# Up products of a gated MLP with the high and low part of the rows as one 512-column moving operand

## The chip, the cores and the metric

The kernel runs on one core of a Trainium2 chip. The metric is device time in microseconds (us): the median of the runs of the whole program.

## The reference, cut to what matters

The program computes a decoder trunk of two layers over 256 rows (T) of width 1024 (D), with d_ff = 2816. Each layer is an attention part (one combined input projection, two attention mixers, two branch products, an output product) followed by a gated MLP with a causal convolution of width 3 behind the up-projection. The change is in the MLP, with two small moves outside it.

```python
def conv_ffn(h, w_up, conv_w, conv_b, w_down):
    u = h @ w_up
    s = u.shape[1]
    up = jnp.pad(u, ((0, 0), (CONV_WIDTH - 1, 0), (0, 0)))
    c = conv_b
    for k in range(CONV_WIDTH):
        c = c + conv_w[k] * up[:, k:k + s]
    a, val = jnp.split(c, 2, axis=-1)
    return (jax.nn.gelu(a, approximate=True) * val) @ w_down

x = x + rms_norm(mix, attn_post_gain)
h = rms_norm(x, ffn_pre_gain)
x = x + rms_norm(conv_ffn(h, ...), ffn_post_gain)
```

## The kernel before, in words

Every float32 product is emulated: each operand is split into a high part (rounded to the engine's fast fp32 form) and a low part (what is left), and three products are summed in PSUM: high·high, high·low and low·high. A weight tile comes by DMA, ScalarE casts its high part `wh` (L114, function `copy`), and VectorE subtracts to get its low part `wl` (L117, `sub`). These pairs `wh`, `wl` stand in a ring of four. A cast into a place of the ring waits for TensorE's last use of the tile that stood there four tiles earlier.

The MLP (`ffn_layer`) has the 2816 inner columns in 22 tiles of 128, numbered j. Each j has two halves (the gate's side and the value's side), each with a weight tile of its own of 8 x 128 x 128.

- j = 0 and 1 are made in another manner (`up_first`, rows as the stationary operand, then transposes).
- For j = 2 to 20: `up(j, 0)`, `up(j, 1)`, then the gate `act_gate`, then `down(j - 2)` for both blocks of 128 rows (t = 0, 1). `up` issues for each of 8 k-steps three matmuls of 256 columns (L1064: wh with the rows' high part `hh`; L1065: wh with the rows' low part `hl`; L1066: wl with `hh`). The result is transposed: 128 inner columns on partitions, 256 rows along the free axis, both halves of a j in one PSUM bank ("T" and "mm" in turn).
- The gate: for each half a convolution, which is one ACT instruction (L1047, scale and bias) and two VectorE instructions (L1050, L1051), all reading PSUM; gelu (L1073, ACT), the product of both halves (L1077, VectorE), the high part `gh` (L114, ACT) and the low part `gl` (L117, VectorE). `gh` and `gl` are the stationary operands of `down`, 12 matmuls of 512 columns for each j (L388 to L390), summed over all j into two banks "S" (t = 0) and two banks "O" (t = 1).
- j = 21 is done last, written out by hand (`manual_schedule`). Then `down` of j = 18 to 21 follows. In layer 0 the hand order stays in force to the end: t = 0 of all four, then t = 1. In the last layer the scheduler orders them.

After the products of a row block comes its norm: ACT squares and sums (L407), VectorE multiplies by the gain (L408) and adds to X (L413). In `out_layer`, ahead of the MLP, L384 squares X for the next norm, L984 scales it, L395 transposes it, and L114/L117 write the transposed rows' high and low parts (`hp`). `W.high(n)` issues a cast of weight tile n and returns the function that issues its low part.

At the start of layer 0, `rope_tables` builds the rotary tables `tab` (8 instructions on GpSimd, L370 and L371, from a cosine and a sine that ACT wrote); L502 and L504 on VectorE multiply q and k with them.

The order of the instructions on each engine is fixed when the program is built (a scheduler's list order except under `manual_schedule`); at run time each engine takes its instructions in that order.

Of the kernel before, what the change touches and what calls it, by code (L numbers as in the profile page):

```python
# [65 lines left out]
def tile_hybrid_trunk(  # L66
# [147 lines left out]
    TAGS = {"kB": 1, "sg": 2, "q8": 3}  # L214
# [71 lines left out]
    last_sq = [None]  # L286

# [60 lines left out]
    def rope_tables():  # L348
        pf = small("r_pf", 2, 1)
        dve.tensor_copy(pf, pos_i)  # L350
        tmp = k1().rearrange("p (i t d) -> p i t d", i=4, t=2)
        r, n, s, c = [tmp[:, i] for i in range(4)]
# [11 lines left out]
        dve.tensor_scalar(n, n, -1.0, math.pi / 2, ALU.mult, ALU.add)  # L364
# [78 lines left out]
    def attn_layer(l, xp, rs, gains, first, order, last_T):  # L443
# [16 lines left out]
        def in_tile(i, tag, fin, tmajor=False, hooks={}):  # L460
# [4 lines left out]
            def go(t, c):  # L465
                if c not in chs:
                    chs[c] = W.next(2, w)
# [93 lines left out]
        qA, qB, qR = big8("q8", 3), big8("q8", 3), big8("q8", 3)  # L561
# [398 lines left out]
        return yp  # L960

    def out_layer(l, yp, gains, order):
# [34 lines left out]
        hp = big8("q8", 3), big8("q8", 3)  # L997
# [29 lines left out]
        return hp, [lambda: t4_of(xg[1], hp, 1, 0), lambda: t4_of(xg[1], hp, 1, 1)]  # L1027


    def ffn_layer(l, hp, gains, last, order, last_T):  # L1030
        hh, hl = hp
# [12 lines left out]
        def conv(b, jj, half, then=None):  # L1044
            c = k1()
            u = b[:, half * T:(half + 1) * T]
# [72 lines left out]
        def up_first_T(t, us):  # L1119
# [97 lines left out]
    def start():  # L1217
# [31 lines left out]
        def rest():  # L1249
# [3 lines left out]
            rope_tables()  # L1253
# [94 lines left out]
```

## Time and profile before

| | |
|---|---|
| device time, median of 3 runs | 774.85 us (774.59 to 775.27) |
| profiled execution | 775.03 us |
| its span in the trace | 773.2 us |
| TensorE busy | 756.6 us, 98% of the span, mean granted clock 0.997 |
| VectorE busy | 611.8 us, 79% |
| ScalarE busy | 495.7 us, 64% |
| GpSimd busy | 33.1 us, 4% |
| MLP loop of layer 0 | 210 to 375.78 us |

The span is what the trace covers; the execution's time is 1.83 us longer. Engines are PE (TensorE matmul), PEld (its weight load), DVE (VectorE), ACT (ScalarE), POOL (GpSimd), SP (SyncE, DMA issue). Matmuls are pipelined, so the duration in a row is longer than the distance from one start to the next; the text counts distances of starts for them. A row of a timeline gives start, duration, engine, line, operation, output<-inputs, form, count, and in brackets how long the engine sat idle before it and who ended that.

### The profile page before, as it was taken

The page shows a single profiled execution, that of the slowest core. Times are in us where ns is not written, and L with a number is a line of the kernel's source. Part 1 is how long each engine was busy: PE and PEld are TensorE (multiplying, and loading weights), DVE is VectorE, ACT ScalarE, POOL GpSimd, SP SyncE. Part 2 cuts the span into 40 slices and gives each one's busy share as a digit, 9 for nine tenths or more (in the row PEclk, how much of TensorE's full clock was granted, in tenths as well). Part 3 has the DMA queues.
Part 4 walks back from the last instruction along what each step waited for, and adds up shares of the span by engine and source line. Part 5 has one row for each costly group of instructions (what it writes and reads, how often), then busy time and mean ns, then how long its engine had stood idle before and what let it go on. Part 6 is the DMA issues. An engine that isn't in the chain of part 4 may idle for free.

```text
span 773.2 us, 12869 instructions
## 1 busy us (share of the span) xinstructions
PE 756.6 (98%) x4742; PEld 676.7 (88%) x4742; DVE 611.8 (79%) x1180; ACT 495.7 (64%) x950; POOL 33.1 (4%) x60
## 2 busy tenths in 40 slices
PE   8999999999999999999999999999999999999996
PEld 6788898888799999999878889988888999999995
DVE  7899898687687777787787989985976876777675
ACT  6596987755565555665566979866565655566552
POOL 4200001000000000000010000010010000000000
PEclk9999999999999999999999999999999999999998
DMA  8624265355566565676335323544655565557631
GB/s 332 205 82 134 68 200 196 133 174 183 190 195 190 189 189 177 224 250 197 131 116 167 97 82 124 202 153 158 198 186 164 186 181 184 188 191 218 202 98 54
DMA packets 42346, 131.26 MB, mean 170 GB/s; under 512 B 5375, under 2 KB 5931, under 8 KB 42283
## 3 DMA queue, kind: packets, MB, share of 16 engines
q1 hardware_dynamic: 41707, 129.39, 51.9%
q10 hardware_dynamic: 576, 1.05, 0.4%
q8 instruction: 37, 0.61, 0.3%
q14 instruction: 26, 0.21, 0.1%
HBM read 129.37 MB, written 1.05 MB: 169 GB/s over the span
## 4 chain that ended last, share of the span: by engine, by line
PE 83%; ACT 8%; DVE 5%; issue 1%; POOL 1%; DMA 1%; SPq 0%; DVEq 0%; POOLq 0%; ACTq 0%
PE mm L388 6%; PE mm L390 6%; PE mm L389 6%; PE mm L1066 5%; PE mm L1065 5%; PE mm L1064 5%; PE S L388 5%; PE S L390 5%; PE S L389 5%; PE T L1065 5%; PE T L1064 5%; PE T L1066 5%; PE O L389 4%; PE O L388 4%; PE O L390 4%; PE T L674 2%
## 5 line engine op out<-in xcount | busy, mean ns | idle before, releaser
L117 DVE TENSOR_TENSOR wl<-st,wh 128x1024 fp32r<-128x1024 f32 (+2 forms) x214 | 253.5, 1185 | 96.0 <-ACT wh L114 95.2
L114 ACT ACTIVATE wh<-st 128x1024 fp32r<-128x1024 f32 (+2 forms) x214 | 218.8, 1027 | 160.5 <-PE mm L1065 39.3
L1064 PE MATMUL mm<-q,wh 128*128 128x256 f32 x336 | 95.1, 283 | 0.0
L1065 PE MATMUL mm<-q,wh 128*128 128x256 f32 x336 | 95.0, 283 | 0.0
L1066 PE MATMUL mm<-q,wl 128*128 128x256 f32 x336 | 95.0, 283 | 0.0
L388 PE MATMUL mm<-wh,x 128*128 128x512 f32 (+2 forms) x240 | 89.6, 373 | 0.7 <-DVE VT L558 0.7
L389 PE MATMUL mm<-wl,x 128*128 128x512 f32 (+2 forms) x240 | 88.3, 368 | 0.0
L390 PE MATMUL mm<-wh,x 128*128 128x512 f32 (+2 forms) x240 | 88.2, 368 | 0.0
L1065 PE MATMUL T<-q,wh 128*128 128x256 f32 x304 | 86.0, 283 | 0.0
L1066 PE MATMUL T<-q,wl 128*128 128x256 f32 x304 | 86.0, 283 | 0.0
L1064 PE MATMUL T<-q,wh 128*128 128x256 f32 x304 | 85.9, 283 | 0.0
L1064 PEld LDWEIGHTS mm<-q,wh 128*128 128x128 f32 x336 | 64.4, 192 | 1.0
L1065 PEld LDWEIGHTS mm<-q,wh 128*128 128x128 f32 x336 | 64.4, 192 | 0.8
L1066 PEld LDWEIGHTS mm<-q,wl 128*128 128x128 f32 x336 | 64.4, 192 | 0.1
L1064 PEld LDWEIGHTS T<-q,wh 128*128 128x128 f32 x304 | 58.3, 192 | 0.8
L1065 PEld LDWEIGHTS T<-q,wh 128*128 128x128 f32 x304 | 58.3, 192 | 0.7
L1066 PEld LDWEIGHTS T<-q,wl 128*128 128x128 f32 x304 | 58.3, 192 | 0.0
L388 PEld LDWEIGHTS mm<-wh,x 128*128 128x128 f32 x240 | 45.2, 188 | 5.7 <-issue 0.9
L390 PEld LDWEIGHTS mm<-wh,x 128*128 128x128 f32 x240 | 45.1, 188 | 5.6 <-DVE x L117 0.4
L389 PEld LDWEIGHTS mm<-wl,x 128*128 128x128 f32 x240 | 45.2, 188 | 4.5
L647 ACT ACTIVATE k<-k,mn 128x128 f32<-128x128 f32 (+1 forms) x96 | 42.4, 445 | 7.2 <-DVE mn L644 7.0
L114 ACT ACTIVATE k<-k 128x256 fp32r<-128x256 f32 x72 | 29.1, 414 | 14.6 <-DVE k L506 6.3
(336 smaller groups left out, 1672.1 us busy)
## 6 DMA issues: line engine op xcount, KB each, us to landing
st<-in_ffn_w_up_dram SPq DMA_DIRECT2D x88, 512.0 KB, 3.9
st<-in_ffn_w_down_dram SPq DMA_DIRECT2D x44, 512.0 KB, 3.6
st<-in_w_in_dram SPq DMA_DIRECT2D x42, 512.0 KB, 3.6
st<-in_w_out_dram SPq DMA_DIRECT2D x16, 512.0 KB, 3.8
st<-in_w_in_dram SPq DMA_DIRECT2D x16, 384.0 KB, 3.1
st<-in_cmp_w_dram SPq DMA_DIRECT2D x16, 256.0 KB, 2.6
st<-in_w_branch_a_dram SPq DMA_DIRECT2D x8, 512.0 KB, 3.6
st<-in_w_branch_b_dram SPq DMA_DIRECT2D x8, 512.0 KB, 3.5
```

The source lines that it names most:

```text
L114: return act.activation(dst, src, AF.Copy, scale=scale)
L117: return dve.tensor_tensor(dst, a, b, ALU.subtract)
L388: pe.matmul(o, xh, wh, start=first, stop=False, skip_group_check=True)
L389: pe.matmul(o, xh, wl, start=False, stop=False, skip_group_check=True)
L390: pe.matmul(o, xl, wh, start=False, stop=last, skip_group_check=True)
L647: last_exp[0] = act.activation(self.pt[:, hh, s, :], sm[:, :nk], AF.Exp, bias=self.mn[:, i:i + 1], scale=-1.0, accum_out=self.dn[:, i:i + 1])
L674: pe.transpose(b[:, i * P:(i + 1) * P], self.pt[:, h, s, kb * P:(kb + 1) * P], ident)
L1064: pe.matmul(o, wh[:, k, :], hh[:, k, c0:c1], start=(k == 0), stop=False, skip_group_check=True)
L1065: pe.matmul(o, wh[:, k, :], hl[:, k, c0:c1], start=False, stop=False, skip_group_check=True)
L1066: pe.matmul(o, wl[:, k, :], hh[:, k, c0:c1], start=False, stop=(k == 7), skip_group_check=True)
```

## The change

1. One tile `H` (128 x 2 x 8 x 256) holds the rows' high part `H[:, 0]` and low part `H[:, 1]`. In `up` each k-step issues one matmul of wh with both, 512 columns (one PSUM bank: columns 0 to 255 take high·high, 256 to 511 take high·low), and one of wl with `hh`, 256 columns into the first half. Each (j, half) has a bank of its own.
2. `left(j, half)`: ACT copies the bank's second half to SBUF, VectorE adds the first half to it. The convolution reads that sum in SBUF. For j = 0 and 1 nothing is added.
3. `act_gate(j)` issues both copies and adds, then both convolutions, then gelu, product, `gh`, `gl`.
4. `out_layer`: the cast of weight tile first+12 (`W.high`) is issued behind the second row block's squares, its low part behind the second transposes.
5. `rope_tables`: three ACT Sin instructions write `tab` themselves and one VectorE instruction makes the scaled pair; the GpSimd instructions are gone. The first weight tiles of in_tile 1 are issued behind that.

```diff
-        def up(j, half, c0, c1):
-            if j not in up_bank:
-                up_bank[j] = bank("T" if j % 4 < 2 else "mm")
+        def up(j, half):
+            b = up_bank[j, half] = bank("mm" if j % 2 == 0 else "T")
...
-            o = up_bank[j][:, half * T + c0:half * T + c1]
+            both = b.rearrange("p (s t) -> p s t", s=2)
             for k in range(8):
-                pe.matmul(o, wh[:, k, :], hh[:, k, c0:c1], start=(k == 0), stop=False, skip_group_check=True)
-                pe.matmul(o, wh[:, k, :], hl[:, k, c0:c1], start=False, stop=False, skip_group_check=True)
-                pe.matmul(o, wl[:, k, :], hh[:, k, c0:c1], start=False, stop=(k == 7), skip_group_check=True)
+                pe.matmul(both, wh[:, k, :], H[:, :, k, :], start=(k == 0), stop=False, skip_group_check=True)
+                pe.matmul(b[:, 0:T], wl[:, k, :], hh[:, k, :], start=False, stop=(k == 7), skip_group_check=True)
...
+        def left(j, half):
+            if j < 2:
+                return up_bank[j][:, half * T:(half + 1) * T]
+            b = up_bank.pop((j, half))
+            u = k1()
+            copy(u, b[:, T:2 * T])
+            dve.tensor_tensor(u, b[:, 0:T], u, ALU.add)
+            return u
+
+        def act_gate(j):
+            ua, uv = left(j, 0), left(j, 1)
+            ca, cv = conv(ua, j), conv(uv, 22 + j)
+            act.activation(ca, ca, AF.Gelu_apprx_tanh)
             dve.tensor_tensor(ca, ca, cv, ALU.mult)
...
-        low = W.high(first + 12)
         for n in range(2):
             norm_b(1, n, g, r)
-        low()
         r = rstd_of(mean_sq(halves(X[:, 1, :])))
+        low = W.high(first + 12)
...
-        act.activation(s, r, AF.Sin)
-        act.activation(c, n, AF.Sin)
-        for i, f in ((0, -SCALE), (2, 1.0)):
-            for h, g in ((0, -f), (1, f)):
-                dd = slice(h * 32, h * 32 + 32)
-                pool.tensor_scalar(tab[:, i, :, dd], c, f, None, ALU.mult)
-                pool.tensor_scalar(tab[:, i + 1, :, dd], s, g, None, ALU.mult)
+        twice = tab[:, 2].rearrange("p t (h d) -> p t h d", h=2)
+        act.activation(twice, c[:, :, None, :].to_broadcast([P, 2, 2, 32]), AF.Sin)
+        act.activation(tab[:, 3, :, 0:32], r, AF.Sin, scale=-1.0)
+        act.activation(tab[:, 3, :, 32:64], r, AF.Sin)
+        return angles, dve.tensor_scalar(tab[:, 0:2], tab[:, 2:4], -SCALE, None, ALU.mult)
```

Three places show how the instructions stand. First ScalarE in the middle of layer 0's MLP loop, before (a period of one j; `wh` rows are casts of weight tiles, `k` rows with L1047 the convolutions, L1073 gelu, the `k<-k` copy is `gh`):

```order
L1047 ACTIVATE k_669_2715<-mm_2654,vec 128x256
L114 ACTIVATE wh_2824<-st_2822 128x1024
L1073 ACTIVATE k_669_2715<-k_669_2715 128x256
L1047 ACTIVATE k_670_2720<-mm_2654,vec 128x256
L114 ACTIVATE wh_2843<-st_2841 128x1024
L114 ACTIVATE k_671_2725<-k_669_2715 128x256
```

And now (the copies out of banks T are `left`; the convolution is L1049, gelu L1081):

```order
L114 ACTIVATE wh_2954<-st_2952 128x1024
L114 ACTIVATE k_702_2848<-T_2802 128x256
L114 ACTIVATE k_703_2851<-T_2825 128x256
L114 ACTIVATE wh_2973<-st_2971 128x1024
L1049 ACTIVATE k_704_2854<-k_702_2848,vec 128x256
L1049 ACTIVATE k_705_2858<-k_703_2851,vec 128x256
L114 ACTIVATE wh_2996<-st_2994 128x1024
L1081 ACTIVATE k_704_2854<-k_704_2854 128x256
L114 ACTIVATE k_706_2864<-k_704_2854 128x256
```

The two copies are new, and the gate's work stands about one cast later against the casts than before. Second, ScalarE at the end of layer 0's MLP, before, from the last cast that waits for TensorE (`wh_4342`) to the last `gh` (`k_934`); the first L1047 is that of j = 20, half 0, L1155 is gelu of j = 21:

```order
L114 ACTIVATE wh_4342<-st_4340 128x1024 [waits DMAHW6_49,PE_49]
L1047 ACTIVATE k_917_4318<-T_4257,vec 128x256 [waits PE_49]
L1073 ACTIVATE k_917_4318<-k_917_4318 128x256 [waits DVE_49,Activation_49]
L1047 ACTIVATE k_918_4323<-T_4257,vec 128x256
L114 ACTIVATE k_919_4328<-k_917_4318 128x256 [waits DVE_49]
L1047 ACTIVATE k_928_4371<-T_4346,vec 128x256 [waits PE_49]
L1155 ACTIVATE k_928_4371<-k_928_4371 128x256 [waits DVE_49,Activation_49]
L1047 ACTIVATE k_930_4401<-mm_4376,vec 128x256 [waits PE_49]
L114 ACTIVATE wh_4405<-st_4403 128x1024
L114 ACTIVATE k_934_4411<-k_928_4371 128x256
```

And now, from j = 19's gate, behind that same cast (here `wh_4160`), through j = 20 (from `k_967`) to the first instruction of j = 21 (`k_980`); the rows of j = 21 go on as copy, convolution, gelu L1158, copy, convolution, a cast, `gh`:

```order
L114 ACTIVATE wh_4160<-st_4158 128x1024 [waits DMAHW6_49,PE_49]
L1049 ACTIVATE k_952_4052<-k_950_4046,vec 128x256 [waits DVE_49]
L1049 ACTIVATE k_953_4056<-k_951_4049,vec 128x256 [waits DVE_49]
L1081 ACTIVATE k_952_4052<-k_952_4052 128x256 [waits DVE_49,Activation_49]
L114 ACTIVATE k_954_4062<-k_952_4052 128x256 [waits DVE_49]
L114 ACTIVATE k_967_4130<-mm_4084 128x256
L114 ACTIVATE k_968_4133<-mm_4107 128x256 [waits PE_49]
L1049 ACTIVATE k_969_4136<-k_967_4130,vec 128x256 [waits DVE_49]
L1049 ACTIVATE k_970_4140<-k_968_4133,vec 128x256 [waits DVE_49]
L1081 ACTIVATE k_969_4136<-k_969_4136 128x256 [waits DVE_49,Activation_49]
L114 ACTIVATE k_971_4146<-k_969_4136 128x256 [waits DVE_49]
L114 ACTIVATE k_980_4181<-T_4164 128x256 [waits PE_49]
```

Behind that cast stood one and a half gates (j = 20 and 21, of which half 0 of j = 20 starts at once); now a gate more (19) stands there. Third, TensorE at the end of the last layer, before (`S` are the banks of t = 0, `O` those of t = 1, `k_1851` is `gh` of j = 21, `k_1811` that of j = 18):

```order
L388 MATMUL O_6962<-wh_8641,k_1811_8447 128x512
L389 MATMUL O_6962<-wl_8642,k_1811_8447 128x512
L390 MATMUL O_6962<-wh_8641,k_1812_8448 128x512
L388 MATMUL O_6963<-wh_8641,k_1811_8447 128x512
L388 MATMUL S_6954<-sg_8261,k_1851_8711 128x512 [waits Activation_49]
```

And now (`k_1945` is `gh` of j = 20, `k_1959` that of j = 21):

```order
L389 MATMUL O_6757<-kB_7756,k_1945_8265 128x512
L390 MATMUL O_6757<-kB_7756,k_1946_8266 128x512
L388 MATMUL S_6748<-sg_7929,k_1959_8333 128x512 [waits Activation_49]
L389 MATMUL S_6748<-sg_7930,k_1959_8333 128x512
L390 MATMUL S_6748<-sg_7929,k_1960_8334 128x512 [waits DVE_49]
L388 MATMUL S_6749<-sg_7929,k_1959_8333 128x512
L389 MATMUL S_6749<-sg_7930,k_1959_8333 128x512
L390 MATMUL S_6749<-sg_7929,k_1960_8334 128x512
L388 MATMUL O_6756<-sg_7929,k_1959_8333 128x512
```

All products of t = 1 for j = 18 to 20 now stand ahead of the first product of j = 21; before, four of them did.

## Rows read from the trace of the kernel before

**Rows 1.** The page's busy times, share of the span, instructions

```profile
PE 756.6 (98%) x4742; PEld 676.7 (88%) x4742; DVE 611.8 (79%) x1180; ACT 495.7 (64%) x950; POOL 33.1 (4%) x60
```

**Rows 2.** Windows, one j of layer 0: us, then busy us by engine, clock, DMA

```profile
242.12:250.65 8.53, 8.53 (x62) 8.01 (x61) 6.19 (x9) 4.72 (x7) 0.00 (x0) 1.00 0.62 185
```

**Rows 3.** Timeline of PE, next j: first product of each run

```profile
250.65 0.39 PE L388 MATMUL S<-wh,k 128*128 128x512 f32 x1
...
253.43 0.28 PE L1064 MATMUL mm<-q,wh 128*128 128x256 f32 x1
...
259.18 0.39 PE L388 MATMUL S<-wh,k 128*128 128x512 f32 x1
```

**Rows 4.** Timeline of PE, long run of 512 columns: first, and the 25th

```profile
14.50 0.39 PE L388 MATMUL mm<-wh,x 128*128 128x512 f32 x1
...
19.94 0.39 PE L388 MATMUL S<-wh,x 128*128 128x512 f32 x1
```

**Rows 5.** Timeline of PE, the dearest single step of 512 columns there

```profile
378.56 0.40 PE L388 MATMUL S<-kB,k 128*128 128x512 f32 x1
378.81 0.40 PE L389 MATMUL S<-kB,k 128*128 128x512 f32 x1
```

**Rows 6.** The page's groups of L1064: count, busy us, mean ns

```profile
L1064 PE MATMUL mm<-q,wh 128*128 128x256 f32 x336 | 95.1, 283 | 0.0
...
L1064 PE MATMUL T<-q,wh 128*128 128x256 f32 x304 | 85.9, 283 | 0.0
```

**Rows 7.** Groups by line, 210 to 364 us: count, busy us, mean ns, idle before

```profile
L117 DVE TENSOR_TENSOR wl<-st,wh 128x1024 fp32r<-128x1024 f32 x55 | 67.3, 1224 | 27.6 <-ACT wh L114 27.5
L114 ACT ACTIVATE wh<-st 128x1024 fp32r<-128x1024 f32 x54 | 57.1, 1058 | 47.8 <-PE mm L1065 19.2 <-PE O L390 15.8 <-PE T L1065 12.9
...
L1047 ACT ACTIVATE k<-mm,vec 128x256 f32<-128x256 f32 x19 | 10.4, 549 | 0.0
L1050 DVE SCALAR_TENSOR_TENSOR k<-mm,vec,k 128x255 f32<-128x255 f32 x19 | 9.1, 478 | 0.0
...
L1077 DVE TENSOR_TENSOR k<-k,k 128x256 f32<-128x256 f32 x19 | 8.1, 425 | 0.7
...
L114 ACT ACTIVATE k<-k 128x256 fp32r<-128x256 f32 x19 | 7.9, 416 | 2.5 <-DVE k L1077 2.4
```

**Rows 8.** Timeline of ACT, end of layer 0's MLP

```profile
370.10 1.06 ACT L114 ACTIVATE wh<-st 128x1024 fp32r<-128x1024 f32 x1 [1.49 <-PE T L1065]
...
380.24 0.42 ACT L114 ACTIVATE k<-k 128x256 fp32r<-128x256 f32 x1 [0.58 <-DVE k L1160]
```

**Rows 9.** Timeline of PE, same stretch

```profile
375.78 0.39 PE L388 MATMUL S<-wh,k 128*128 128x512 f32 x1
...
380.70 0.51 PE L388 MATMUL S<-sg,k 128*128 128x512 f32 x1 [0.58 <-ACT k L114]
```

**Rows 10.** Timeline of PE, end of the last layer

```profile
755.61 0.39 PE L388 MATMUL S<-wh,k 128*128 128x512 f32 x1
...
766.55 0.40 PE L390 MATMUL O<-sg,k 128*128 128x512 f32 x1
```

**Rows 11.** Timeline of DVE, end of the last layer

```profile
762.36 1.39 DVE L408 TENSOR_TENSOR k<-S,gain 128x512 f32<-128x512 f32 x2 [1.44 <-ACT k L407]
764.10 1.41 DVE L413 SCALAR_TENSOR_TENSOR X<-k,rstd,X 128x512 f32<-128x512 f32 x2 [0.34 <-POOL rstd L377]
...
768.73 1.41 DVE L413 SCALAR_TENSOR_TENSOR X<-k,rstd,X 128x512 f32<-128x512 f32 x2 [0.33 <-POOL rstd L377]
```

**Rows 12.** Timeline of ACT, end of layer 0's out_layer

```profile
198.88 1.05 ACT L114 ACTIVATE wh<-st 128x1024 fp32r<-128x1024 f32 x1
199.83 0.61 ACT L384 ACTIVATE k<-X 128x512 f32<-128x512 f32 x1
```

**Rows 13.** Timeline of PE, same stretch

```profile
203.10 0.63 PE L395 MATMUL T<-cst,k 128*128 128x128 f32 x4 [0.94 <-DVE k L984]
```

**Rows 14.** Timeline of POOL, rotary tables

```profile
23.86 1.35 POOL L370 TENSOR_SCALAR tab<-k 128x64 f32<-128x64 f32 x4
```

**Rows 15.** Timeline of DVE, first use of the tables

```profile
24.59 0.75 DVE L502 SCALAR_TENSOR_TENSOR k<-mm,rstd,tab 128x512 f32<-128x512 f32 x1 [1.59 <-POOL tab L370]
```

More of the change, by code (lines that the diff above doesn't have):

```diff
@@ L212, in next @@
             return self.made[self.used - 1]
-    TAGS = {"kB": 1, "sg": 2, "q8": 3}
+    TAGS = {"kB": 1, "sg": 2, "q8": 1}
     W = Stream()
@@ L286, in tile_hybrid_trunk @@
     last_sq = [None]
+    tables = []
     def table(fn):
@@ L351, in rope_tables @@
         tmp = k1().rearrange("p (i t d) -> p i t d", i=4, t=2)
-        r, n, s, c = [tmp[:, i] for i in range(4)]
+        r, n, c = [tmp[:, i] for i in range(3)]
         for t in range(2):
@@ L363, in rope_tables @@
         dve.scalar_tensor_tensor(n, r, -1.0, r, ALU.mult, ALU.max)
[L364 to L371 removed]
+        angles = dve.tensor_scalar(c, n, -1.0, math.pi / 2, ALU.mult, ALU.add)
+        twice = tab[:, 2].rearrange("p t (h d) -> p t h d", h=2)
[3 more added lines that the diff above has]
+        return angles, dve.tensor_scalar(tab[:, 0:2], tab[:, 2:4], -SCALE, None, ALU.mult)
     def rstd_of(s2):
@@ L466, in go @@
                 if c not in chs:
-                    chs[c] = W.next(2, w)
+                    with tc.issue_after(tables[c > 0].ins) if first and i == 1 else nullcontext():
+                        chs[c] = W.next(2, w)
                 ch = chs[c]
@@ L559, in v_split @@
             done.update(keys)
-        qA, qB, qR = big8("q8", 3), big8("q8", 3), big8("q8", 3)
+        H = ap_.tile([P, 2, KD, T], F32R, tag="h16", name=nm("H"))
+        qA, qB, qR = H[:, 0], H[:, 1], big8("q8", 1)
         kA = ap_.tile([P, 2, 2, T], F32R, tag="kA", name=nm("kA"))
@@ L959, in attn_layer, with out_layer @@
         branch(1)
-        return yp
-    def out_layer(l, yp, gains, order):
+        return yp, H
+    def out_layer(l, yp, H, gains, order):
         gains["ffn_pre"] = gain_tile(ffn_pre_gain, l)
@@ L996, in out_layer @@
             product(0, [k])
-        hp = big8("q8", 3), big8("q8", 3)
+        hp = H[:, 0], H[:, 1]
         g, r = norm_a(res[0], gp)
@@ L1019, in out_layer, with ffn_layer @@
             table(AF.Gelu_apprx_tanh)
-        low = W.high(first + 12)
         for n in range(2):
             norm_b(1, n, g, r)
-        low()
         r = rstd_of(mean_sq(halves(X[:, 1, :])))
+        low = W.high(first + 12)
         xg[1] = k4()
         scaled(1, r)
-        return hp, [lambda: t4_of(xg[1], hp, 1, 0), lambda: t4_of(xg[1], hp, 1, 1)]
-    def ffn_layer(l, hp, gains, last, order, last_T):
-        hh, hl = hp
+        return [lambda: t4_of(xg[1], hp, 1, 0), lambda: (t4_of(xg[1], hp, 1, 1), low())]
+    def ffn_layer(l, H, gains, last, order, last_T):
+        hh, hl = hp = H[:, 0], H[:, 1]
         gains["ffn_post"] = gain_tile(ffn_post_gain, l)
@@ L1042, in ffn_layer, with conv @@
         lows = []
-        def conv(b, jj, half, then=None):
+        def conv(u, jj, then=None):
             c = k1()
-            u = b[:, half * T:(half + 1) * T]
             act.activation(c, u, AF.Identity, bias=cb(l, jj), scale=cw(l, 2, jj))
@@ L1127, in up_first_T @@
                 for j in range(2):
-                    for half in range(2):
-                        act_gate(j, half)
+                    act_gate(j)
         for t in range(2):
@@ L1137, in ffn_layer @@
             for half in range(2):
-                part(lambda: up(j, half, 0, T))
-            for half in range(2):
-                act_gate(j, half)
+                part(lambda: up(j, half))
+            act_gate(j)
             if j in (NJ - 8, NJ - 6):
@@ L1152, in ffn_layer @@
             W.ensure(early[l, k])
-        part(lambda: up(j, 0, 0, T))
-        ca = conv(up_bank.pop(j), j, 0)
+        part(lambda: up(j, 0))
+        ca = conv(left(j, 0), j)
         act.activation(ca, ca, AF.Gelu_apprx_tanh)
-        up_bank[j] = bank("mm")
-        part(lambda: up(j, 1, 0, T))
+        part(lambda: up(j, 1))
         nxt = None if last else [early[l + 1, "in", c] for c in range(4)]
-        cv = conv(up_bank.pop(j), 22 + j, 1, None if last else lambda: lows.append(W.high(nxt[2])))
+        cv = conv(left(j, 1), 22 + j, None if last else lambda: lows.append(W.high(nxt[2])))
         dve.tensor_tensor(ca, ca, cv, ALU.mult)
@@ L1252, in rest @@
             dve.tensor_scalar(nsink, sink, -1.0, None, ALU.mult)
-            rope_tables()
+            tables.extend(rope_tables())
             table(AF.Exp)
@@ L1264, in tile_hybrid_trunk @@
     for l in range(DEPTH):
-        yp = attn_layer(l, xp, rs, gains, l == 0, order, last_T)
-        hp, last_T = out_layer(l, yp, gains, order)
-        xp, rs, last_T = ffn_layer(l, hp, gains, l == DEPTH - 1, order, last_T)
+        yp, H = attn_layer(l, xp, rs, gains, l == 0, order, last_T)
+        last_T = out_layer(l, yp, H, gains, order)
+        xp, rs, last_T = ffn_layer(l, H, gains, l == DEPTH - 1, order, last_T)
     idle(50)
```

10 lines of the change are left out of this document (1 added, 9 removed).

## The prediction

> **What bounds the kernel now.** I read the busy times first: TensorE is busy 98% of the span, VectorE 79%, ScalarE 64% [rows 1]. Then the window of one j in the middle of layer 0's MLP: in 8.53 us TensorE is busy all 8.53, VectorE 6.19, ScalarE 4.72, at clock 1.00 [rows 2]. In the loop TensorE is the bound; the others only have to keep up. Then TensorE's starts there: 12 matmuls of 512 columns in 2.78 us (0.2317 each) and 48 of 256 columns in 5.75 us (0.1198 each) [rows 3]. Two matmuls of 256 columns (0.2396) thus cost more than one of 512. Last I read the loop's ends, where no more products cover the gate: in layer 0 the first product of j = 21 sat 0.58 us idle for `gh` [rows 9], and behind the last layer's products come only norm work and the output [rows 10, 11].
>
> **The pair of products.** The groups of L1064 count 336 + 304 = 640 k-steps in both layers [rows 6]. A step costs 3 x 0.1198 = 0.3594 now, and then one step of 512 plus 0.1198. No run of the trace alternates 512 with 256, so the 512 has bounds: 0.2267 in a long run (24 in 5.44 us) [rows 4], and 0.25, the dearest single one seen [rows 5]. The nearest row is the loop's own block, 0.2317 [rows 3], beside the same casts and transfers; its operand, though, is a weight tile new to each block. I take the middle of 0.2267 and 0.2317, 0.2292. Saved: 640 x (0.3594 - 0.3490) = 6.7 us; bounds: 640 x (0.3594 - 0.3465) = 8.3 saved, 640 x (0.3698 - 0.3594) = 6.7 lost.
>
> The rows say that a matmul's fixed part here is 2 x 0.1198 - 0.2267 = 0.013 us [rows 3, 4]. The Trainium skill, page "TensorE: Matmul & The Clock Gate", section "Back-to-back issue gap", gives the gap of a lone matmul as N/2.4 plus 2.5 ns, which speaks against this change: 640 matmuls fewer would then save an estimated 640 x 2.5 ns = 1.6 us, and the sum below would lie 5 us higher. These rows contradict its fixed part for this data type by a factor of five.
>
> **New work in the loop.** For each j: two copies on ScalarE and two adds on VectorE, about 0.42 us each [rows 7]. ScalarE comes to 4.72 + 0.84 = 5.6 and VectorE to 6.19 + 0.85 = 7.0 of a period of 16 x 0.349 + 2.78 = 8.36 us. TensorE covers both: nothing. If that cover goes, see the second rival. The halves go into banks of their own, and the next use of such a bank is two j later for its half: I charge 0.2 us once, at j = 21, where no `down` stands between.
>
> **The end of layer 0's loop.** Let E0 be the end of up(20, 1); before, the cast that waits for it started at 370.10 [rows 8] and half 0 of j = 20's convolution right behind it. Now, behind that cast stand the convolutions of j = 19, and all of j = 20 and 21 behind those. I add durations [rows 7], with ScalarE and VectorE alternating: cast 1.06; VectorE's `wl` 1.22 and four convolution steps of 0.48 to E0 + 4.3; gelu, product, `gh`(19), 0.42 each, to E0 + 5.2 (gelu starts a step early and overlaps). j = 20: copy, add, convolution 0.55 to E0 + 6.7 (the second pair runs beside it), four steps to E0 + 8.7, product and `gh`(20) to E0 + 9.6. j = 21, half by half: copy, add, convolution, two steps, gelu to E0 + 12.4; copy, add, convolution, two steps, product, `gh`(21) to E0 + 15.8.
> TensorE: two ups of 8 x 0.349 and the 0.2 end at E0 + 5.8; `down` of j = 18 and 19 for t = 0 (six matmuls, 1.39 each) at E0 + 8.6; `down` of 20 waits 1.0 for `gh`(20) and ends at E0 + 11.0; `down` of 21 waits 4.8. By hand order nothing of t = 1 may go ahead. With the 0.2, that is 6.0 us. Before, three `down` from 375.78 end at 379.95 and the fourth started at 380.70, so 0.75 was lost [rows 9]. Net +5.1 us. Bounds: +3.9 if each of some fourteen hand-offs overlaps by 0.08 as neighbouring instructions of one engine do (in [rows 12] a cast of 1.05 has the next start 0.95 behind), +6.3 if each costs 0.08 more.
>
> **The end of the last layer.** `gh`(21) again comes at E0 + 15.8, which is E + 10.0 when E is the end of the ups. TensorE may do 36 matmuls first (8.35 us), waits 1.6, and ends the 12 of j = 21 at E + 12.8; before it ended at 766.78, 755.61 + 11.17 [rows 10]. More counts behind it: before, the norm of t = 0 ran under the products of t = 1 (L408 at 762.36, L413 at 764.10 [rows 11]). Now both halves' norms come together: VectorE's four L408 and four L413 make 2 x 1.39 + 2 x 1.41 = 5.6 us, from about E + 11.6 (first bank of S done at E + 10.7, its squares 0.8) to E + 17.2. Before, the last L413 ended at 770.14, E + 14.53. Net +2.7 us; bounds +1.6 (TensorE's delay alone) and +3.5.
>
> **Moves outside.** In out_layer the cast that stood ahead of the squares took 0.95 us from its start to theirs [rows 12]; behind them it can delay nothing on TensorE until the second transposes, which waited 0.94 us [rows 13]. Its low part moves likewise, to after the transposes, and is needed only at the MLP's later weights. X is ready some time in that 0.95: bounds 0 and 0.95 for each layer, taken 0.45, so -0.9. The tables: VectorE sat 1.59 us idle for GpSimd's last writes [rows 14, 15]. The new form takes one VectorE instruction and a third Sin, so between 0 and 1.6 saved, taken 0.8. The DMA issue swapped with it waits for the tables, early enough for in_tile 1: nothing.
>
> **Sum.** -6.7 + 5.1 + 2.7 - 0.9 - 0.8 = -0.6 us against the profiled execution's 775.03, so 774.4; the median of the runs shown lies 0.18 lower, so **774.2 us**. A difference of 0.2%, 1.55 us, is about what a measurement of this kernel can tell from no change.
>
> **The rivals.**
> 1. *The pair runs at the long run's pitch and the ends are cheaper* (faster). For it: `H` lies still in SBUF as the operand of the long run did, and layer 0's chain by overlapping starts is 3.9. Against: beside the casts the 512 took 0.2317. Then -8.3 + 3.9 + 2 - 1.5 = -3.9: 771.0 us.
> 2. *The gate's loop becomes the bound* (slower). One round through VectorE and ScalarE (three `wl` of 1.22, two adds, four steps, product, `gh`, and the next cast, whose `wl` waits for it) is 3.67 + 0.85 + 1.92 + 0.43 + 0.42 + 1.06 = 8.35 by durations; with four hand-offs of 0.08 it is 8.7. It decides from a round of 8.36 on. At 8.7, 38 gates cost 0.3 each, 12 us: 786. Against: by distances of starts instead of durations, 0.1 less for each of ten instructions, it is 7.7, and now the engines idle long for TensorE (47.8 us ahead of casts [rows 7]).
> 3. *The two halves save nothing as one operand* (slower): 512 columns in two pieces cost what two matmuls do. Then only +6.7 of the sum above falls away: 780.9 us. This is what the fixed part of the Trainium skill's page would nearly make of it. Against: [rows 3, 4].
> 4. *A pair costs the dearest step throughout*, 0.3698: 774.2 + 13.4 = 788. Against: that step occurs once, at a change of operands.
> 5. *The ends cost more*, as nothing shows new waits on banks: +3 us, 777 us.
>
> **How the numbers follow.** The forecast (771.9 to 776.5) has 0.42, of which 0.14 lies below 773.3 and 0.28 within 0.2%. Rival 1 has 0.30, rival 2 0.08, rival 3 0.06, rival 4 0.04, rival 5 0.10 (0.03 of it within). Faster: 0.14 + 0.30 = 0.44. Same: 0.28 + 0.03 = 0.31. Slower: 0.08 + 0.06 + 0.04 + 0.07 = 0.25. The range takes in rivals 1 and 5 and leaves out 2 to 4: 770.5 to 779.0 us.
>
> **What would show it.** In the profile after: a k-step of `up` from start to start (0.349); TensorE without idle time inside the loop; its waits ahead of `down` of 20 and 21 in layer 0 (1.0 and 4.8) and ahead of that of 21 in the last layer (1.6); the last L413's end against the end of the ups (17.2); the wait ahead of L395 (0.5) and of L502 (0.8). The forecast is wrong if a k-step is over 0.352 or under 0.345, or if TensorE idles in every j.

## The result, and the profile after

The change makes the kernel slower: median 778.69 us (778.39 to 780.75) against 775.27 for the kernel before on the same chip, ratio 1.0053 (95% interval 1.0042 to 1.0064). A later measurement of the same two kernels gave 779.17 us against 774.91. The time lies in the forecast range (770.5 to 779.0), but on the wrong side of the kernel before: the forecast was 774.2, and faster had been given 0.44, slower 0.25.

The profiled execution took 780.75 us, with a span of 779.0, 5.8 us longer than the span before. The busy times, to be held against [rows 1]:

```profile
PE 757.1 (97%) x4102; PEld 645.9 (83%) x4102; DVE 632.5 (81%) x1261; ACT 520.8 (67%) x1031; POOL 27.3 (4%) x52
```

640 matmuls fewer, and yet TensorE is busy as long as before: 0.5 us longer. So part of its work has become slower. The waits of TensorE's queue by cause (us in total, times, longest) name the place where it also stands idle:

```profile
PE S L388 <- ACT k L114: 6.2, 3, 4.6
...
PE T L395 <- DVE k L988: 1.0, 2, 0.5
```

The first row is `down` waiting for `gh`; before, there was one such wait, of 0.58 [rows 9]. The second is the wait that the moved cast shortens (before 0.93 and 0.94 [rows 13], now twice 0.5). TensorE's timeline at the end of layer 0's MLP, from the first product of `down` (t = 0) on:

```profile
374.26 0.39 PE L388 MATMUL S<-wh,k 128*128 128x512 f32 x1
...
377.69 0.50 PE L388 MATMUL S<-kB,k 128*128 128x512 f32 x1 [0.48 <-ACT k L114]
...
378.95 0.40 PE L390 MATMUL S<-kB,k 128*128 128x512 f32 x1
383.97 0.80 PE L388 MATMUL S<-sg,k 128*128 128x512 f32 x1 [4.62 <-ACT k L114]
384.56 0.63 PE L389 MATMUL S<-sg,k 128*128 128x512 f32 x1
...
389.25 0.42 PE L388 MATMUL O<-wh,k 128*128 128x512 f32 x1
389.51 0.39 PE L389 MATMUL O<-wl,k 128*128 128x512 f32 x1
```

The waits of 0.48 and 4.62 us are those for `gh`(20) and `gh`(21), where 1.0 and 4.8 were forecast. New is what stands behind them: twelve products from 383.97 to 389.25, 5.28 us, where twelve took 2.78 before [rows 3]. The windows of the same profile (us, then busy by engine, granted clock, DMA) say why:

```profile
50.00:52.00 2.00, 1.22 (x8) 1.01 (x7) 1.99 (x9) 2.00 (x7) 0.00 (x0) 0.85 0.00 0
52.00:54.00 2.00, 2.00 (x11) 1.99 (x11) 1.63 (x11) 1.35 (x5) 0.00 (x0) 0.50 0.00 0
...
380.00:385.00 5.00, 1.03 (x3) 0.85 (x4) 2.96 (x7) 3.59 (x6) 0.00 (x0) 0.75 0.00 0
385.00:390.00 5.00, 5.00 (x15) 3.94 (x14) 4.20 (x6) 1.89 (x5) 0.86 (x2) 0.57 0.60 194
```

During and behind the idle stretch the granted clock falls to 0.50, the 1.2 GHz level, and returns to 1.00 at about 389 us. That costs 5.28 - 2.78 = 2.5 us. The Trainium skill, page "TensorE: Matmul & The Clock Gate", section "What's actually happening", describes a clock that idling lowers; the trace agrees, with 0.50 behind 4.62 us without a product. The first two rows show such a stretch at 52 us as well; below it turns out to come in some executions only.

ScalarE's timeline there shows the chain that `gh`(21) hangs on. To be held against [rows 8]:

```profile
368.36 1.06 ACT L114 ACTIVATE wh<-st 128x1024 fp32r<-128x1024 f32 x1 [0.93 <-PE mm L1066]
369.32 1.08 ACT L1049 ACTIVATE k<-k,vec 128x256 f32<-128x256 f32 x2
...
373.19 0.64 ACT L114 ACTIVATE k<-mm 128x256 f32<-128x256 f32 x2
...
377.54 0.36 ACT L114 ACTIVATE k<-T 128x256 f32<-128x256 f32 x1
...
383.50 0.42 ACT L114 ACTIVATE k<-k 128x256 fp32r<-128x256 f32 x1 [0.58 <-DVE k L1162]
```

The cast, then the convolutions of j = 19; the copies of j = 20 at 373.19; the first copy of j = 21 at 377.54; `gh`(21) at 383.50. With E the end of the ups, `gh`(21) stood at E + 4.5 before (380.24 - 375.78) and stands at E + 9.2 now (383.50 - 374.26).

The last layer ends like this (TensorE's last wait, VectorE's norm work):

```profile
768.13 0.51 PE L388 MATMUL S<-sg,k 128*128 128x512 f32 x1 [1.13 <-ACT k L114]
```

```profile
769.86 1.38 DVE L408 TENSOR_TENSOR k<-S,gain 128x512 f32<-128x512 f32 x2 [1.33 <-ACT k L407]
771.60 1.42 DVE L413 SCALAR_TENSOR_TENSOR X<-k,rstd,X 128x512 f32<-128x512 f32 x2 [0.35 <-POOL rstd L377]
772.94 1.27 DVE L408 TENSOR_TENSOR k<-O,gain 128x512 f32<-128x512 f32 x2
774.14 1.40 DVE L413 SCALAR_TENSOR_TENSOR X<-k,rstd,X 128x512 f32<-128x512 f32 x2
```

Both halves' norms now run one after the other: 775.54 - 758.49 = 17.05 us behind the ups, against 14.53 before [rows 10, 11].

The loop itself did what it should. Two stretches of 14 k-steps of `up` without a wait, in layer 0 and in the last layer:

```profile
369.05 0.40 PE L1066 MATMUL T<-H,wh 128*128 128x512 f32 x1
...
373.90 0.40 PE L1066 MATMUL T<-H,wh 128*128 128x512 f32 x1
...
753.20 0.40 PE L1066 MATMUL T<-H,wh 128*128 128x512 f32 x1
...
758.14 0.40 PE L1066 MATMUL T<-H,wh 128*128 128x512 f32 x1
```

4.85 / 14 = 0.346 and 4.94 / 14 = 0.353 us for a k-step; over the 597 steps that follow each other with nothing in between the mean is 0.351 (before, over 598, 0.360).

By stages, between marks of both traces: the L395 of [rows 13] and the same one in layer 1, the end E of the ups (375.78 and 755.61 before, 374.26 and 758.49 after), and the first L395 behind E in layer 0. The marks that stand nowhere above, before and then after:

```profile
386.39 0.60 PE L395 MATMUL T<-cst,k 128*128 128x128 f32 x4
...
582.93 0.63 PE L395 MATMUL T<-cst,k 128*128 128x128 f32 x4 [0.93 <-DVE k L984]
```

```profile
203.87 0.63 PE L395 MATMUL T<-cst,k 128*128 128x128 f32 x4 [0.52 <-DVE k L988]
...
392.06 0.60 PE L395 MATMUL T<-cst,k 128*128 128x128 f32 x4
...
588.00 0.63 PE L395 MATMUL T<-cst,k 128*128 128x128 f32 x4 [0.51 <-DVE k L988]
...
758.49 0.40 PE L389 MATMUL S<-wl,k 128*128 128x512 f32 x1
```

| stretch | before | after | difference |
|---|---|---|---|
| L395 of [rows 13] to E, layer 0 | 172.68 | 170.39 | -2.3 |
| E to the next L395 | 10.61 | 17.80 | +7.2 |
| that L395 to the marked one of layer 1 | 196.54 | 195.94 | -0.6 |
| from there to E, layer 1 | 172.68 | 170.49 | -2.2 |
| E to the end of the last L413 | 14.53 | 17.05 | +2.5 |

The two loops gain 4.5 us, their ends lose 9.7. (Ahead of the first mark this profile is 0.8 us later, with the stretch of lower clock at 52 us in it.) In the second profile of the same kernel, taken below, the five differences are -2.2, +6.2, +0.1, -2.2 and +2.5: loops and the last end repeat, the second and third stretch differ by 1.0 and 0.7 us from one execution to the next.

### The profile page after: what moved, and what is told of

The parts are those of the page before. It is cut to its first block, busy times and chain, and to the rows that moved or that the text cites. A ratio compares the mean times of both kernels' runs of the same rounds, so it can differ in the third digit from the quotient of the medians.

```text
span 779.0 us, 11862 instructions
## 1 busy us (share of the span) xinstructions
PE 757.1 (97%) x4102; PEld 645.9 (83%) x4102; DVE 632.5 (81%) x1261; ACT 520.8 (67%) x1031; POOL 27.3 (4%) x52
## 3 DMA queue, kind: packets, MB, share of 16 engines
q10 hardware_dynamic: 576, 1.05, 0.4%
HBM read 129.37 MB, written 1.05 MB: 167 GB/s over the span
## 4 chain that ended last, share of the span: by engine, by line
PE 83%; ACT 8%; DVE 5%; issue 1%; DMA 1%; POOL 1%; SPq 0%; DVEq 0%; ACTq 0%
PE mm L1066 10%; PE T L1066 8%; PE mm L388 6%; PE mm L389 6%; PE mm L390 6%; PE S L388 5%; PE S L390 5%; PE S L389 5%; PE mm L1067 5%; PE T L1067 4%; PE O L389 3%; PE O L390 3%; PE O L388 3%; PE T L678 2%; ACT k L651 2%; ACT k L114 2%
## 5 line engine op out<-in xcount | busy, mean ns | idle before, releaser
L1066 PE MATMUL mm<-H,wh 128*128 128x512 f32 x320 | 114.0, 399 | 0.0
L1066 PE MATMUL T<-H,wh 128*128 128x512 f32 x320 | 112.5, 393 | 0.2 <-DVE k L1075 0.2
L1067 PE MATMUL mm<-H,wl 128*128 128x256 f32 x320 | 89.8, 281 | 0.0
L1067 PE MATMUL T<-H,wl 128*128 128x256 f32 x320 | 89.5, 280 | 0.0
L1066 PEld LDWEIGHTS mm<-H,wh 128*128 128x128 f32 x320 | 60.1, 188 | 14.7
L1066 PEld LDWEIGHTS T<-H,wh 128*128 128x128 f32 x320 | 59.9, 187 | 14.3 <-PE mm L1067 0.7
L1067 PEld LDWEIGHTS T<-H,wl 128*128 128x128 f32 x320 | 60.4, 189 | 1.0
L1067 PEld LDWEIGHTS mm<-H,wl 128*128 128x128 f32 x320 | 60.4, 189 | 0.8
L1049 ACT ACTIVATE k<-k,vec 128x256 f32<-128x256 f32 x80 | 43.4, 588 | 2.7 <-DVE k L1075 2.7
L1052 DVE SCALAR_TENSOR_TENSOR k<-k,vec,k 128x255 f32<-128x255 f32 x80 | 35.3, 478 | 3.4 <-ACT k L1049 3.4
```

Of the source, the lines that this page charges most:

```text
L1049: act.activation(c, u, AF.Identity, bias=cb(l, jj), scale=cw(l, 2, jj))
L1052: dve.scalar_tensor_tensor(c[:, 1:T], u[:, 0:T - 1], cw(l, 1, jj), c[:, 1:T], ALU.mult, ALU.add)
L1066: pe.matmul(both, wh[:, k, :], H[:, :, k, :], start=(k == 0), stop=False, skip_group_check=True)
L1067: pe.matmul(b[:, 0:T], wl[:, k, :], hh[:, k, :], start=False, stop=(k == 7), skip_group_check=True)
```

## The experiments

The theory: the pairs gain in the loop; the added copies and adds make the last gates late; what TensorE waits there costs a second time by the clock. Rivals: the pairs gain nothing; putting both convolutions first is to blame; the outer parts cost; the clock has another cause.

**The clock, by itself.** Products that nobody reads fill the wait:

```diff
-        downs(0, js)
+        downs(0, js[:3])
+        zb = bank("mm")
+        for _ in range(19):
+            pe.matmul(zb.rearrange("p (s t) -> p s t", s=2), H[:, 0, 0, 0:P], H[:, :, 0, :], start=True, stop=True, skip_group_check=True)
+        downs(0, js[3:])
```

> The changed kernel with 19 further matmuls of 512 columns (operands at hand, into a bank nobody reads) between down of j = 20 and down of j = 21, t = 0, at the end of layer 0's MLP: 19 x 0.229 = 4.4 us, about the 4.62 us that TensorE waits there for gh(21). They do none of the kernel's work. Theory (the wait of 4.62 us costs twice, once as idle time and once more because the clock is at its lower level for the products behind it): the granted clock stays at 1.00 from 374 to 394 us, gh(21) is no earlier, the products behind it take 0.23 us each instead of 0.43, and the time falls by about 2.2 us against the changed kernel, to 776.3. Rival (the lower clock there has another cause, or the norm behind it sets the time): no change, 778.5.

Measured 776.82 us, ratio to before 1.0025 (1.0015 to 1.0035). The row of `down` of j = 21, and the windows:

```profile
382.27 0.51 PE L388 MATMUL S<-sg,k 128*128 128x512 f32 x1 [0.33 <-ACT k L114]
```

```profile
380.00:385.00 5.00, 4.67 (x21) 3.45 (x20) 4.15 (x7) 3.97 (x8) 0.24 (x1) 1.00 0.06 8
385.00:390.00 5.00, 5.00 (x26) 4.05 (x25) 4.38 (x7) 2.50 (x7) 1.54 (x4) 1.00 0.58 202
```

`gh`(21) is as late as ever, but the clock stays at 1.00, and 778.69 - 776.82 = 1.9 us come back by doing more work. The lower clock behind the wait is shown to be a cost of its own.

**The old form for the last three gates** (`up_old` is `up` of the kernel before):

```diff
+            if j >= 19:
+                return up_old(j, half)
...
-            if j < 2:
+            if j < 2 or j >= 19:
                 return up_bank[j][:, half * T:(half + 1) * T]
...
+            if j >= 19:
+                ca = conv(left(j, 0), j)
+                act.activation(ca, ca, AF.Gelu_apprx_tanh)
+                cv = conv(left(j, 1), 22 + j)
...
```

> The changed kernel with j = 19, 20 and 21 made in the old manner in both layers (three products of 256 columns for each k-step, convolution straight out of PSUM, no copy, no add, a half's convolution, then gelu, then the other half's). Theory (the pairs gain, the longer gate behind the last cast loses it at the ends of both loops): TensorE's waits for gh(20) and gh(21) in layer 0 fall from 0.48 + 4.62 to below 0.9 us, the clock stays at 1.00 there, the last layer's end is 14.5 us behind the ups again; 778.5 - 4.3 (waits) - 2.2 (clock) - 2.5 (last layer) + 0.9 (96 of 640 k-steps at 0.359 instead of 0.350) = 770.4 us. Rival (the pairs gain nothing in the loop, or the new copies and adds cost there): not below 774.

Measured 769.51 us, ratio 0.993 (0.9914 to 0.9947): faster than both kernels. One wait is left:

```profile
377.73 0.50 PE L388 MATMUL S<-sg,k 128*128 128x512 f32 x1 [0.90 <-ACT k L114]
```

```profile
380.00:385.00 5.00, 5.00 (x25) 4.09 (x24) 4.38 (x8) 2.15 (x8) 1.32 (x4) 1.00 0.62 210
```

17 of 20 j in the new form keep the gain, and the ends are those of before: the last L413 ended 14.5 us behind the ups. The rival that the pairs gain nothing falls.

**No copies, no adds:**

```diff
-            u = k1()
-            copy(u, b[:, T:2 * T])
-            dve.tensor_tensor(u, b[:, 0:T], u, ALU.add)
-            return u
+            return b[:, 0:T]
```

> The changed kernel without the copies and adds: the convolution reads the first half of the bank in PSUM, so the high-low product is made by TensorE but left out of the sum. Theory: ScalarE's order at the end of layer 0 is again that of the kernel before (two copies fewer for each gate, one gate less behind the last cast), waits below 1 us, clock up, the last layer's end 14.5 us behind the ups; what is left is the pairs' gain (640 x 0.009 = 5.7) and the outer parts' (1.0 measured): 774.9 - 5.7 - 1.0 = 768.2 us. Rival (the pairs' results are late for other reasons, as a bank for each half): 772 or more.

Measured 768.08 us, ratio 0.9913 (0.9898 to 0.9928). No wait of `down` for `gh` is among TensorE's waits at all. So the copies and adds, not the pairs or their banks, carry the loss: 778.69 - 768.08 = 10.6 us.

**Both convolutions first, alone in the kernel before:**

```diff
-            if half == 0:
-                ca = ga[j] = conv(up_bank[j], j, 0)
-                act.activation(ca, ca, AF.Gelu_apprx_tanh)
-                return
-            ca = ga.pop(j)
+            if half == 0:
+                return
+            ca = conv(up_bank[j], j, 0)
             cv = conv(up_bank.pop(j), 22 + j, 1)
+            act.activation(ca, ca, AF.Gelu_apprx_tanh)
...
```

> The kernel before with only the third part of the change: of each j's gate both convolutions first (out of PSUM, as before), then gelu, product, gh, gl. Theory (the loss at the ends of the loops comes from the copies and adds, which set the gate behind the cast that waits for up(20, 1)): ScalarE's order at the end of layer 0 stays that of the kernel before but for gelu behind the second convolution; waits there below 1 us, time within 0.5 us of 774.9. Rival (putting both convolutions first is what makes the last gate late): 2 us or more slower than before, 777 and up, with a wait of over 2 us for gh(21).

Measured 774.66 us, ratio 0.9999 (0.999 to 1.0009): no difference.

**And undone in the changed kernel:**

```diff
-            ua, uv = left(j, 0), left(j, 1)
-            ca, cv = conv(ua, j), conv(uv, 22 + j)
-            act.activation(ca, ca, AF.Gelu_apprx_tanh)
+            ca = conv(left(j, 0), j)
+            act.activation(ca, ca, AF.Gelu_apprx_tanh)
+            cv = conv(left(j, 1), 22 + j)
```

> The changed kernel with the gate half by half again: copy, add, convolution, gelu of half 0, then copy, add, convolution of half 1. Theory (copies and adds, not the order of the convolutions): the gate of j = 19 still stands behind the cast that waits for up(20, 1), waits of about 0.5 and 4.6 us for gh(20) and gh(21), clock down behind them, time 778 to 779. Rival (both convolutions first is the cause): waits below 1 us, 771 us.

Measured 788.79 us, ratio 1.0181 (1.0166 to 1.0196): a miss for both. The sum of `down`'s waits, and three of them, two in the middle of the loop and one for `gh`(20):

```profile
PE S L388 <- ACT k L114: 12.8, 9, 4.6
```

```profile
326.24 0.50 PE L388 MATMUL S<-wh,k 128*128 128x512 f32 x1 [1.33 <-ACT k L114]
...
345.75 0.50 PE L388 MATMUL S<-wh,k 128*128 128x512 f32 x1 [1.33 <-ACT k L114]
...
381.82 0.50 PE L388 MATMUL S<-kB,k 128*128 128x512 f32 x1 [1.71 <-ACT k L114]
```

The gate now falls behind TensorE inside the loop too, four times in layer 0 (3.2 us) and twice in layer 1 (0.5 us). ScalarE's rows ahead of the wait at 326.24 show why:

```profile
324.82 1.06 ACT L114 ACTIVATE wh<-st 128x1024 fp32r<-128x1024 f32 x1 [1.71 <-PE T L1066]
325.78 0.40 ACT L114 ACTIVATE k<-k 128x256 fp32r<-128x256 f32 x1
```

`gh` stands directly behind a cast that itself waits 1.71 us for TensorE; ahead of the wait at 345.75 it is the same. So these two have the cause of the loop's end, a gate behind a cast that waits for an `up`, in another place of the order. Both convolutions first gain nothing in the kernel before, but with the copies they are worth 10 us.

**Where the lateness comes from.** Three parts can be read from the traces. up(21, 0) starts at 370.02 before and at 368.63 now. Behind that, j = 20's first convolution started 1.05 us later before; the copies of j = 20 start 4.6 later now: 3.5 us for the place of gate 19. From there to the first instruction of j = 21's gate it took 5.1 us before and takes 4.4 now, as both halves of j = 20 run side by side: 0.7 us less. And from that instruction to the end of `gh`(21) it took 4.5 us (376.15 to 380.66), now 6.4 (377.54 to 383.92): 1.9 us. Together that is the 4.7 us by which `gh`(21) is later against the ups. First a hand order for gate 19:

```diff
+            if j == NJ - 3:
+                order.enter_context(tc.manual_schedule(engines=MANUAL0))
             for half in range(2):
                 part(lambda: up(j, half))
+                if j == NJ - 2:
+                    W.ensure(early[l, NJ - 4 + half])
+            if j == NJ - 3:
+                n = W.used
+                W.ensure(n + 2)
+                W.ensure(n + 3)
             act_gate(j)
+            if j == NJ - 3:
+                W.ensure(n + 4)
...
```

> The changed kernel with nothing left out, but with a hand order from j = 19 on: the gate of j = 19 ahead of the casts of up(21, 1) and of down's weights of 18 and 19, so that behind the cast that waits for up(20, 1) stand only the gates of 20 and 21, as before. Theory (the place of gate 19 costs more than the length of a gate): gh(20) at 6.3 us and gh(21) at about 12.2 us behind the end of up(20, 1), so no wait for down of 20 and about 2.2 us for down of 21 in layer 0, none for it in the last layer; if the clock stays up behind 2.2 us: 778.5 - 2.9 - 2.2 - 2.0 = 771.4 us; if it falls all the same, 773.5. Rival (the longer gates themselves make it late wherever they stand): 776 or more.

Measured 779.48 us, ratio 1.0063 (1.0048 to 1.0078): a miss for the theory. ScalarE's timeline shows why; up(21, 0) starts at 367.98 there:

```profile
368.64 0.42 ACT L114 ACTIVATE k<-k 128x256 fp32r<-128x256 f32 x1 [1.03 <-DVE k L1082]
368.96 2.94 ACT L114 ACTIVATE wh<-st 128x1024 fp32r<-128x1024 f32 x3
371.81 0.36 ACT L114 ACTIVATE k<-mm 128x256 f32<-128x256 f32 x1
```

Gate 18 had kept gate 19 waiting until 364.5, so `gh`(19) came only at 368.64, and three casts of 2.94 us then stood ahead of j = 20's copies. VectorE's three `wl` held the adds until 373.46, and gate 20 was as late as before the edit. The time fits the rival (776 or more), but the run does not speak for it: it moved the obstacle and did not test its price. A cleaner test takes gate 19 alone back to the old form:

```diff
+        OLD = (19,)
...
-            if j < 2:
+            if j < 2 or j in OLD:
                 return up_bank[j][:, half * T:(half + 1) * T]
```

> The changed kernel with j = 19 alone in the old manner (256 columns, no copies), j = 20 and 21 in the new. Theory (the last gh is late by the sum of two things: 3.4 us because the gate of j = 19 stands behind the cast that waits for up(20, 1), and 1.8 us because the gate of j = 21 itself is longer by two copies and adds): gate 20 follows that cast at once, gh(21) comes about 12.6 us behind the end of up(20, 1) instead of 15.2, TensorE waits 2.8 us for it and not at all for gh(20); the last layer's end falls from 17.0 to about 14.8 us behind the ups. Time: 778.5 - 2.3 - 2.2 (clock, if it stays up behind 2.8 us) - 2.2 + 0.3 = 772.1 us, 773.6 if the clock falls. Rival (each gate's own length decides, so one shorter gate gives one gate's difference only): wait of 4 us, 777 us.

Measured 774.19 us, ratio 0.9989 (0.998 to 0.9998). With `OLD = (19, 20)`:

> The changed kernel with j = 19 and 20 in the old manner, j = 21 in the new. Theory (as for the run with j = 19 alone): the first convolution of j = 21 as early as in the kernel before, 6.1 us behind the end of up(20, 1), but the gate of 21 takes 6.3 instead of 4.5 us: wait of about 2.7 us for gh(21), against 0.9 with 19 to 21 old and 4.6 with none: 769.5 + 1.8 (layer 0) - 0.3, and up to 0.5 in the last layer: 771 to 771.5, 1.5 more if the clock falls behind such a wait. Rival (the new gate of 21 is not what is long): 769.5.

Measured 773.38 us, ratio 0.9982 (0.9973 to 0.9991). The rows of `down` of j = 21, with 19 alone in the old form, and with 19 and 20:

```profile
379.82 0.79 PE L388 MATMUL S<-sg,k 128*128 128x512 f32 x1 [2.99 <-ACT k L114]
```

```profile
379.65 0.63 PE L388 MATMUL S<-sg,k 128*128 128x512 f32 x1 [2.91 <-ACT k L114]
```

The waits are 2.99 and 2.91 us, where 2.8 and 2.7 were expected, and there is none for `gh`(20). Step by step: with all three gates in the new form `down` waits 0.48 + 4.62 us, with 19 in the old form 2.99, with 19 and 20 2.91, with all three 0.90. So gate 19 costs 2.1 us of waits, gate 20 nearly nothing and gate 21 2.0. For gate 19 the run does not part its place from its length, as the old form changes both. The clock falls behind waits of this length too (the window of the first of the two), and with that in the sums, 773.6 and 772.5 to 773, the times lie 0.4 to 0.9 us above them:

```profile
380.00:385.00 5.00, 5.00 (x17) 3.99 (x18) 4.24 (x6) 2.09 (x5) 0.86 (x2) 0.72 0.49 135
```

**Filling the wait with real work:** `down` of 18 to 20 for t = 1 first.

```diff
-        downs(0, js)
+        downs(0, js[:3])
+        downs(1, js[:3])
+        downs(0, js[3:])
         update(0, *norm_a(banks[0], gains["ffn_post"]))
-        downs(1, js[:3])
```

> The changed kernel with down of j = 18 to 20 for t = 1 ahead of down of j = 21 for t = 0 in layer 0, as the scheduler does in the last layer. Theory: TensorE's wait of 4.62 us is filled with 4.2 us of products and the clock stays up until then; but the norm of t = 0 then has only one product block to hide behind, and TensorE waits about 3 us for the transposes after it; the next layer starts earlier by what the clock cost, or less if the clock falls there: 776 to 778. Rival (the idle time is what counts, and filled it is won): 778.5 - 4.2 - 2.2 = 772.

Measured 778.02 us (776.62 to 779.87), ratio 1.0042 (1.0026 to 1.0058).

```profile
382.11 0.50 PE L388 MATMUL S<-sg,k 128*128 128x512 f32 x1 [0.44 <-ACT k L114]
...
387.52 1.09 PE L395 MATMUL T<-cst,k 128*128 128x128 f32 x4 [3.75 <-DVE k L427]
```

The wait only moves: 4.2 us of products now lie ahead of `gh`(21), and are missing behind it, where the transposes wait 3.75 us for the norm. The clock falls behind that wait instead:

```profile
387.52:390.11 2.59, 2.59 (x8) 2.21 (x9) 1.90 (x3) 1.31 (x4) 1.04 (x3) 0.50 0.21 81
```

**The outer parts**, both in the kernel before, and then the moved cast alone:

```diff
-        low = W.high(first + 12)
         for n in range(2):
             norm_b(1, n, g, r)
-        low()
         r = rstd_of(mean_sq(halves(X[:, 1, :])))
+        low = W.high(first + 12)
...
```

> The kernel before with only the two outer parts of the change: the rotary tables by ScalarE's Sin and one VectorE instruction, and the cast of weight tile first+12 behind the squares. Theory (both are small gains that stay): the wait ahead of L395 falls from 0.94 to 0.5 us in both layers, VectorE's wait for the tables is gone; 775.3 - 0.8 - 0.8 = 773.7 us. Rival (the tables' part brings waits in the attention of layer 0 that let the clock fall, and with it the gain): 774.5 to 776, with a clock below 1.00 between 45 and 60 us.

> The kernel before with only the move of the cast of weight tile first+12 behind the squares, the rotary tables as before. Theory: the wait ahead of L395 falls from 0.94 to 0.5 us twice: 774.8 - 0.85 = 774.0 us, with runs as close together as those of the kernel before (the two outer parts together had runs of 773.5 to 774.1 and some at 775.0 to 775.3; the latter come from the tables' part). Rival (the gain of both parts came from the tables): 774.8, or a spread as with both.

Both: 773.94 us (773.53 to 775.33), ratio 0.9991 (0.9982 to 1.0). The cast alone: 773.94 (773.81 to 774.16), ratio 0.9988 (0.9979 to 0.9997). The cast gives the whole 1.0 us. The tables give nothing in the median, and with them three of ten runs took 775.0 to 775.3.

**The changed kernel once more:**

> The changed kernel itself once more, for a profile and its spread. Theory: the stretch of lower clock between 51 and 55 us in the profile on record belongs to some executions alone (the one profiled was the slowest, 780.75); another profile shows 1.00 there and the lower clock only behind the wait of 4.62 us; 778.5 us. Rival (the lower clock at 51 us is part of the change): it is there again, and 780.7.

Measured 779.17 us (777.84 to 780.53). The profile has, for 50 to 60 us and for the end of layer 0's MLP:

```profile
50.00:60.00 10.00, 9.22 (x75) 8.91 (x74) 9.62 (x34) 9.96 (x33) 0.00 (x0) 1.00 0.15 52
...
380.00:385.00 5.00, 2.69 (x7) 2.15 (x8) 4.11 (x7) 3.32 (x7) 0.00 (x0) 0.76 0.03 7
385.00:390.00 5.00, 5.00 (x23) 3.99 (x23) 4.08 (x6) 2.13 (x6) 1.11 (x3) 0.89 0.61 203
```

The fall at 52 us is gone; the one behind the wait for `gh`(21) is there again, though shorter. So the first comes in some executions only (the profile first shown was one, that of the hand order for gate 19 another; the other nine profiles with the new tables and the three with the old do not have it), and the second belongs to the change. That the tables raise the odds of the first is suggested by these profiles and by the spread with the tables, and not shown.

## Why the prediction was wrong

The forecast difference was -0.6 us, the measured one +3.4. Two steps of the sum failed, by about the same amount, and the tables gave nothing; the other terms held.

- **The sum lacked a term.** The step that failed is "The end of layer 0's loop": it priced TensorE's waits at what they last. The waits themselves were near: net +4.7 us (E to L395, 17.80 - 10.61 = 7.19, less 2.5 for the clock) against 5.1 forecast (the prediction's own figures, 6.0 - 0.75, make 5.25). That the clock falls behind a wait of 4.6 us had no place in the sum. It costs 1.9 us in the medians (778.69 against 776.82 with the wait filled) and 2.5 in the profile shown. The profile before gave no instance of it: the wait there was 0.58 us [rows 9], with the clock at 1.00.
- **The pairs were oversized.** The other step that failed is "The pair of products": forecast 6.7 us, measured 2.3 + 2.2 between marks. The k-step went from 0.360 to 0.351, which makes 640 x 0.0084 = 5.4 us; 0.351 is 0.002 more than taken, though inside the bounds and nearer to the loop's row. The other 0.9 us was lost between the steps. 0.2 is the wait of up(21, 0) at 368.63 for the add that frees its bank, as charged elsewhere in the sum. 0.2 is one product of `down` (752.42) that stands ahead of the last ups of layer 1 and is missing behind them. 0.5 lies in the products of `down` inside the loops, which take 100.6 us instead of 100.1 from start to start; the run without copies and adds has 0.4 of that as well, and why is open. Without copies and adds the two loops are 5.4 us shorter than before (170.07 and 169.85 us against 172.68 twice).
- **The end of the last layer** was right: +2.5 us against 2.7, for the reason given (both norms one behind the other).
- **The moved cast** was right: 1.0 us against 0.9. **The tables** were not: 0.8 forecast, nothing measured. VectorE's wait for them is gone, and so is TensorE's of 0.99 us at 29.47 before; but in the profile after the transposes at 48.23 and 51.11 us wait 0.57 and 0.78 us, where before 0.17 and, at 52.21, 0.66 were lost.
- **The rivals.** The first fell with the k-step, which did not run at the long run's pitch, and with the ends, which were not cheaper. The second (gate's loop as the bound) was rightly held improbable: no `down` waits inside the loop; in the order half by half two long waits there come from `gh`'s place behind a waiting cast, which the rival's sum of durations does not contain. The third and fourth are refuted by the k-step of 0.351. The fourth's 0.25 us was not even the dearest step of the trace before (217.88 to 218.22 is 0.34), but such steps come single. The fifth (ends dearer by 3 us, 777) came nearest in size, but not for its reason: the wait on banks was the 0.2 us already charged, and clock, pairs and tables made the difference. As the range reached up to 779.0 to take in that rival, it is in part luck that the time fell inside it.
- **The sign.** With the terms as measured: -4.5 + 4.7 + 2.5 + 1.9 - 1.0 = +3.6 us; measured 778.69 - 775.27 = +3.4. Neither failed step alone makes the difference: each moves the forecast by some 2 us.

## What to carry to other kernels

A change that pays in a loop's steady state by adding work to a side chain can lose it again where the loop ends, because there nothing covers that chain. Price the last rounds by themselves, and try the old form for them: here the old form in the last three of 20 rounds gave 769.51 instead of 778.69 us. An idle stretch of TensorE can have a second price, the lower clock on the products behind it; here it came behind waits of 2.9 us and more at the loop's end. And work moved ahead of a wait is taken from the cover of the next one, as the run that filled the wait with `down`'s own products shows.

## What the runs showed of the hardware

- At the end of layer 0's loop the granted clock fell to 0.50 behind waits of 4.62, 3.75, 2.99 and 2.91 us, and stayed at 1.00 behind 0.90 and 0.58. The length of one wait does not tell all: at 51 us of two profiles it fell behind waits of 0.57 and 0.78 us, and in nine others with like waits there it stayed at 1.00. The lower level lasted 9 to 12 products of 512 columns behind the wait of 4.6 us in the two profiles of the changed kernel, so its price varies by about 1 us between executions of one kernel.
- A matmul of 512 columns between matmuls of 256 costs about what it costs among its like: 0.351 us for the pair on average (0.346 and 0.353 in two stretches), where the sum is 0.2267 + 0.1198 = 0.3465 with the long run's step and 0.2317 + 0.1198 = 0.3515 with the loop's own [rows 3, 4].
